# Token-first input stage and fp32 scan state in a one-core decoder trunk

## The chip, the cores and the metric

The kernel runs on one core of a Trainium2 chip, as a single launch. The time is that of the device, in microseconds (us), from start to end of one execution; the number given for the kernel before is the median of three runs, 1500.3 us (1499.67 to 1504.1). The profile is one further execution, recorded by the hardware profiler. TensorE multiplies matrices, VectorE, ScalarE and GpSimd work on rows of tiles, SyncE only issues DMA transfers. Tiles lie in on-chip memory as 128 partitions by a free dimension; TensorE's results lie in a small accumulator memory of banks, each 128 x 512 fp32.

## What is computed

x has 1024 tokens of 1024 channels. One Mamba-2 layer, then one attention layer, both conditioned by a vector c of 1024 numbers. Cut to the two places of the change, input modulation and chunked scan:

```python
def _modulate(x, g, shift, scale):
    return _rmsnorm(x, g) * (1.0 + scale[:, None, :]) + shift[:, None, :]

c_act = jax.nn.silu(c)
shift, scale, gate = jnp.split(c_act @ ada_w[i] + ada_b[i], 3, axis=-1)
h = _modulate(x, norm_g[i], shift, scale)        # rmsnorm: x / sqrt(mean over channels of x*x + eps)
zxbcdt = h @ in_w                                # z 2048, x/B/C 3072 (conv + silu), dt 32
...
def step(state, inp):                            # one chunk of 128 tokens; 4 groups of 8 heads of 64
    xc, ac, bc, cc = inp
    acum = jnp.cumsum(ac, axis=1)
    seg = jnp.where(causal, acum[:, :, None] - acum[:, None, :], -jnp.inf)
    scores = jnp.einsum('btgn,bsgn->btsg', cc, bc)[..., None] * jnp.exp(seg)
    y_diag = jnp.einsum('btsgh,bsghp->btghp', scores, xc)
    y_off = jnp.einsum('btgn,bghpn->btghp', cc, state) * jnp.exp(acum)[..., None]
    w_end = jnp.exp(acum[:, -1:] - acum)
    new_state = (state * jnp.exp(acum[:, -1])[..., None, None]
                 + jnp.einsum('bsgn,bsghp->bghpn', bc, xc * w_end[..., None]))
    return new_state, y_diag + y_off
```

Behind the scan come skip, gate by silu(z), a norm per group of 512 channels, the output projection, one projection to keys and values, stick-breaking attention and a last norm.

## The kernel before

**Numbers in two halves.** A projection in full accuracy runs as three products in the type fp32r (mm3, L129 to L132): an operand is split into a high half (the value rounded to fp32r) and a low half (value minus high), and high by high, low by high and high by low are added in one accumulator bank. Where an operand is plain fp32, a product is one instruction in the program and two records in the trace.

**First stage (L156 to L329).** x comes transposed (xT: tiles of 128 channels by 512 tokens, name x, sixteen of them, eight for each half of the tokens, hf). For the norm, ScalarE squares a tile (squares, L210), VectorE adds pairs (square_add, L215), and TensorE multiplies by a matrix of ones (square_sum, L219, bank ssx), which leaves the sum over channels in every partition; a logarithm, an exponential and three VectorE steps of 512 columns make the row of 1/rms (rms, L140 to L147, tile rbx). GpSimd multiplies each x tile by this row (scaled, L251). c goes through SiLU as an 8 x 128 tile, out to a buffer in memory (c_d) and back as a row crow, the same in all 128 partitions. For each of eight channel tiles d, gemv (L227) makes shift and scale with two VectorE products of 128 x 1024 that sum as they go (tile a0, 1 MB each by DMA); bias (L246, L248) finishes them with two one-column steps of ScalarE. Then high (L257, L260) makes the modulated tile hx and its high half h0h on ScalarE, and low (L265) the low half h0l on VectorE. With both halves of a tile, wave_mm runs nine products (three column tiles by three) into the banks prw; the weights (ww) are split by split_w (L233 on ScalarE, L234 on VectorE for d = 0, on GpSimd for the others). In this stage the order of TensorE, VectorE, ScalarE and GpSimd is the order in which the code is written (manual_schedule, L177). All of SyncE's transfers wait in the order of the program.

**Convolution stage.** The other 21 column tiles of the projection run over all 1024 tokens (bank pr, line 130 and following); its first product needs every tile of the first stage.

**Scan (L446 to L649).** 32 chunks: 8 units (a half of the tokens by a group g) of 4 chunks each. The four groups of the first half go first, then those of the second. For the chunk that comes next, chunk_a loads lm and eb, makes lm = exp of the decays on ScalarE, transposes x (px) and B (pb), multiplies B by C into the second part of pb, and forms xd = x * dt and lm = lm * scores on VectorE. chunk_c makes xw = x * w_end, splits it (xwh, xwl) and splits the transposed B (bsh, bsl). chunk_b runs on TensorE the state product (ps, three fp32r products), yo from the state st, and yd, eight small fp32 products; VectorE multiplies yo by eb, and the state becomes st * decay (GpSimd, in place) + ps (VectorE, L563). The last steps of a unit are gate (L576: skip, L581, gate by sz, squares) and norm_store (L594). Between these, TensorE works on the projection z of the next unit (zproj, 8 steps of three products, bank pz). In this stage only TensorE's order is that of the code (L456); the order of the other engines comes from the scheduler. px, ps, yo and yd have one accumulator bank each, pb two.

## Time and profile before

| | us |
|---|---|
| median of three runs | 1500.3 |
| lowest, highest | 1499.67, 1504.1 |
| the profiled execution, own time | 1502.42 |
| its span, first to last instruction | 1500.7 |
| TensorE busy in the span | 1435.7 (96%) |
| VectorE, ScalarE, GpSimd busy | 991.1, 742.3, 582.6 |
| granted TensorE clock, mean | 0.988 |

The span runs from the first to the last recorded instruction; the execution's own time has 1.7 us more around it. The program goes through its stages one behind the other: first stage to 90.15 us, convolution to 359.8, scan to 624.9, then a stretch of 48.9 us in which the output projection begins, then the rest. Busy shares of the whole span are means over these; a stage is read from its own window. The granted clock is a share of TensorE's full speed, 2.4 GHz; the lower level, 1.2 GHz, stands as about 0.5.

### The profile page before, as it was taken

The page shows a single profiled execution, that of the slowest core. Times are in us where ns is not written, and L with a number is a line of the kernel's source. Part 1 is how long each engine was busy: PE and PEld are TensorE (multiplying, and loading weights), DVE is VectorE, ACT ScalarE, POOL GpSimd, SP SyncE. Part 2 cuts the span into 40 slices and gives each one's busy share as a digit, 9 for nine tenths or more (in the row PEclk, how much of TensorE's full clock was granted, in tenths as well). Part 3 has the DMA queues.
Part 4 walks back from the last instruction along what each step waited for, and adds up shares of the span by engine and source line. Part 5 has one row for each costly group of instructions (what it writes and reads, how often), then busy time and mean ns, then how long its engine had stood idle before and what let it go on. Part 6 is the DMA issues. An engine that isn't in the chain of part 4 may idle for free.

```text
span 1500.7 us, 20592 instructions
## 1 busy us (share of the span) xinstructions
PE 1435.7 (96%) x7538; PEld 1115.1 (74%) x7538; DVE 991.1 (66%) x1221; ACT 742.3 (49%) x1249; POOL 582.6 (39%) x645
## 2 busy tenths in 40 slices
PE   4799999999998999999999999999999999999997
PEld 2587887888876778878888888876666666666797
DVE  5989975455789888886643526416666666668564
ACT  5554346224667666744432424325545455556452
POOL 2821220001654666443111000027666666667532
PEclk8899999999999999999999999999999999999999
DMA  9268885224576666657533446450212211112253
GB/s 333 95 235 295 288 288 170 98 99 122 176 229 198 220 199 210 226 179 264 176 125 124 136 129 194 138 178 33 66 43 64 63 57 39 61 57 78 79 189 106
DMA packets 104581, 227.36 MB, mean 152 GB/s; under 512 B 9488, under 2 KB 40992, under 8 KB 103456
## 3 DMA queue, kind: packets, MB, share of 16 engines
q1 hardware_dynamic: 104480, 226.04, 45.7%
q8 instruction: 60, 0.98, 0.3%
q14 instruction: 41, 0.34, 0.1%
HBM read 184.32 MB, written 41.68 MB: 151 GB/s over the span
## 4 chain that ended last, share of the span: by engine, by line
PE 73%; DVE 5%; ACT 2%; DMA 2%; issue 1%; POOL 1%; DVEq 0%; SPq 0%; POOLq 0%; ACTq 0%
PE sc L835 5%; PE av L888 4%; PE at L867 4%; PE po L132 4%; PE po L130 4%; PE po L131 4%; PE pz L130 2%; PE pqz L130 2%; PE pq L130 2%; PE pz L132 2%; PE pz L131 2%; PE pr L132 2%; PE pq L132 2%; PE pr L130 2%; PE pr L131 2%; PE pq L131 2%
## 5 line engine op out<-in xcount | busy, mean ns | idle before, releaser
L858 POOL TENSOR_TENSOR be<-be,kp 128x1024 f32<-128x1024 f32 (+2 forms) x96 | 162.3, 1691 | 90.2 <-DVE kp L852 70.9
L838 ACT ACTIVATE kp<-sc 128x1024 f32<-128x1024 f32 (+2 forms) x96 | 75.5, 813 | 174.6 <-PE sc L835 172.0
L852 DVE TENSOR_TENSOR_SCAN kp<-kp,pone 128x128 f32<-128x128 f32 (+3 forms) x128 | 96.1, 803 | 69.2 <-POOL kp L845 69.2
L130 PE MATMUL pr<-h0h,hx 128*128 128x512 f32 x336 | 132.3, 394 | 5.0 <-ACT hx L124 2.7
L132 PE MATMUL pr<-h0h,lx 128*128 128x512 f32 x336 | 132.3, 394 | 0.7 <-DVE lx L125 0.7
L131 PE MATMUL pr<-h0l,hx 128*128 128x512 f32 x336 | 131.9, 393 | 0.0
L505 ACT ACTIVATE lm<-lm,nac 128x128 f32<-128x128 f32 x256 | 78.6, 389 | 61.5 <-POOL lm L502 61.4
L130 PE MATMUL pz<-h0h,hz 128*128 128x512 f32 x256 | 105.5, 412 | 0.0
L131 PE MATMUL po<-yl,ho 128*128 128x512 f32 x256 | 100.8, 394 | 1.2 <-DVE yl L665 1.2
L132 PE MATMUL po<-yh,lo 128*128 128x512 f32 x256 | 100.4, 392 | 1.3 <-DVE lo L125 1.3
L132 PE MATMUL pz<-h0h,lz 128*128 128x512 f32 x256 | 100.4, 392 | 1.2 <-DVE lz L125 1.2
L131 PE MATMUL pz<-h0l,hz 128*128 128x512 f32 x256 | 99.9, 390 | 0.0
L130 PE MATMUL po<-yh,ho 128*128 128x512 f32 x256 | 99.9, 391 | 0.0
L852 DVE TENSOR_TENSOR_SCAN kp<-kp,ab,pone 128x512 f32<-128x512 f32 x64 | 78.4, 1266 | 28.3 <-ACT kp L838 17.2
L125 POOL TENSOR_TENSOR lq<-rq,hq 128x256 fp32r<-128x256 f32 x32 | 22.4, 730 | 178.4 <-ACT hq L124 178.4
L533 POOL TENSOR_TENSOR xwl<-xw,xwh 128x512 fp32r<-128x512 f32 x20 | 27.4, 1368 | 160.7 <-ACT xwh L531 156.2
L835 PE MATMUL sc<-kd,q 64*128 64x512 f32 (+3 forms) x384 | 81.5, 522 | 0.8 <-ACT be L839 0.8
L340 DVE SCALAR_TENSOR_TENSOR cv<-pr,vt,cv 128x1023 f32<-128x1023 f32 (+2 forms) x63 | 80.4, 1278 | 0.9
L130 PEld LDWEIGHTS pr<-h0h,hx 128*128 128x128 f32 x336 | 63.8, 190 | 18.9 <-ACT hx L124 3.1
L124 ACT CAST ho<-ro 128x1024 fp32r<-128x1024 f32 x32 | 33.7, 1054 | 89.1 <-PE po L131 79.2
L353 POOL TENSOR_TENSOR ar<-ar,crow 128x1024 f32<-128x1024 f32 x12 | 30.9, 2572 | 119.5 <-DMA ar<-adar 119.5
L867 PE MATMUL at<-ident,be 128*128 128x128 f32 x576 | 74.7, 272 | 1.1 <-DVE aT L877 1.1
(259 smaller groups left out, 3951.7 us busy)
## 6 DMA issues: line engine op xcount, KB each, us to landing
ar<-adar SPq DMA_DIRECT2D x48, 512.0 KB, 5.0
lm<-ac_d SPq DMA_DIRECT2D x32, 512.0 KB, 4.5
rz<-wz SPq DMA_DIRECT2D x32, 512.0 KB, 3.7
ro<-wmo SPq DMA_DIRECT2D x32, 512.0 KB, 3.5
xs_d<-sv SPq DMA_DIRECT2D x24, 512.0 KB, 3.8
rx<-wxbc SPq DMA_DIRECT2D x21, 512.0 KB, 4.7
x<-xT SPq DMA_DIRECT2D x32, 256.0 KB, 5.6
a<-ada SPq DMA_DIRECT2D x8, 1024.0 KB, 7.7
```

Of the source, the lines that this page charges most:

```text
L124: S.copy(h[:, i:i + n, :], r[:, i:i + n, :])
L130: E.matmul(ps, wh, xh, start=first, stop=False)
L131: E.matmul(ps, wh, xl, start=False, stop=False)
L132: E.matmul(ps, wl, xh, start=False, stop=last)
L340: V.scalar_tensor_tensor(out=ac[:, i:], in0=ps[:, :T - i], scalar=vv("cw", m * 4 + 3 - i), in1=ac[:, i:], op0=ALU.mult, op1=ALU.add)
L505: S.activation(lm[:, h, :], lm[:, h, :], AF.Exp, bias=nac[:, c, h0_ + h:h0_ + h + 1])
L835: E.matmul(ps[:, a, o:o + w], q[hsl[a], i * P:(i + 1) * P], kd[hsl[a], HT * c:HT * c + w], start=True, stop=True)
L838: S.activation(kp[:, :, ok:ok + w], ps[:, :, o:o + w], AF.Sigmoid, scale=-0.125)
L852: V.tensor_tensor_scan(out=ka, data0=ka, data1=pone.to_broadcast([P, w]), initial=1.0 if top else above[p, i][:, a, 0:1], op0=ALU.mult, op ...
L858: Q.tensor_tensor(out=be[:, :, o:o + w], in0=be[:, :, o:o + w], in1=kp[:, :, ok + 1:ok + w + 1], op=ALU.mult)
L867: E.transpose(ps[:, j, :], be[:, a, j * P:(j + 1) * P], ident)
L888: E.matmul(ps[hsl[a], cs], vd[:, j, hsl[a]], at[j // 4][:, a, j % 4, cs], start=j == 0, stop=j == nj - 1)
```

## The change

It touches two stages; the stages behind them keep their code and order.

**First stage.** x comes as it is, in tiles of 128 tokens by 1024 channels (xN, new input; names x0 to x7). A token is a partition, so the sum of squares of a token is one instruction with a running sum (squares: even tiles on ScalarE, odd on VectorE), 1/rms is a column of 128 x 4 for each half, and scaled multiplies a whole tile by a column, on VectorE and ScalarE in turn. GpSimd no longer works in this stage. After scaling, turn transposes four 128 x 128 blocks on TensorE into a bank, from which high reads. c is broadcast directly into crow, 512 KB, as the second transfer, and SiLU is taken on the whole row. spin puts products of raw x with the identity on TensorE, whose result is never read. The order of the loop over d is written anew, and split_w is VectorE's everywhere.

**Scan.** The state product is one fp32 product of the unsplit xw and B; xw has two tiles in turn and is made in chunk_a, as is the copy of B. The new state goes through a separate tile sd = st * decay on GpSimd. In chunk_b the order is now yd, yo, state product.

```diff
-        Y.dma_start(out=c8, in_=c)
-        S.activation(c8, c8, AF.Silu)
...
+        load_x(range(1))
+        Y.dma_start(out=crow, in_=c.rearrange("j p -> (j p)").partition_broadcast(P))
+        load_x(range(1, CPH))
...
+        def squares(t):
+            sq = tp.tile([P, D], F32, tag="sq", name=f"sq{t}", bufs=2)
+            acc = ssq[:, t // CPH, t % CPH:t % CPH + 1]
+            if t % 2:
+                V.scalar_tensor_tensor(out=sq, in0=xn[t], scalar=1.0, in1=xn[t], op0=ALU.mult,
+                                       op1=ALU.mult, accum_out=acc)
+            else:
+                S.activation(sq, xn[t], AF.Square, accum_out=acc)
...
+        def spin(x, m):
+            for i in range(m):
+                E.matmul(wave[NW - 1][:, HT:], ident, x, start=True, stop=True)
...
+            inv_rms(ssq[:, hf], rst[:, hf], rtt[:, hf], D)
...
+        def scaled(t):
+            r = rst[:, t // CPH, t % CPH:t % CPH + 1]
+            if t % 2:
+                V.tensor_scalar(out=xn[t], in0=xn[t], scalar1=r, scalar2=None, op0=ALU.mult)
+            else:
+                S.activation(xn[t], xn[t], AF.Identity, scale=r)
...
-        def scaled(d, hf):
-            Q.tensor_tensor(out=xt[d][hf], in0=xt[d][hf], in1=rbs[hf], op=ALU.mult)
...
+        def turn(d, hf):
+            ps = mm_tile(f"xp{d}_{hf}")
+            for i in range(CPH):
+                E.transpose(ps[:, i * P:(i + 1) * P], xn[hf * CPH + i][:, d * P:(d + 1) * P], ident)
+            xps[d, hf] = ps
...
+        squares(0)
+        squares(1)
+        S.activation(crow, crow, AF.Silu)
...
+        for t in range(2, CPH):
+            squares(t)
+        for t in range(CPH):
+            spin(xn[t][:, 0:HT], 2 if t == 0 else 1)
         rms(0)
+        for t in range(CPH):
+            scaled(t)
+        turn(0, 0)
+        turn(1, 0)
+        spin(xn[0][:, 0:HT], 3)
+        split_w(0, V)
         gemv(0)
...
+        unit(0, 0)
         wave_mm(0, 0)
+        spin(xn[0][:, 0:HT], 3)
+        for t in range(CPH, NC_):
+            squares(t)
+        rms(1)
+        for t in range(CPH, NC_):
+            scaled(t)
+        turn(0, 1)
...
         for d in range(2, ND):
...
+            unit(d, 0)
+            turn(d, 1)
+            if d + 1 < ND:
+                gemv(d + 1)
+                split_w(d + 1, V)
+            wave_mm(d, 0)
+            unit(d, 1)
+            if d + 1 < ND:
+                turn(d + 1, 0)
+                bias(d + 1)
+            wave_mm(d, 1)
...
-                xh = py.tile([P, 512], F32R, tag="xwh", name="xwh" + n, bufs=1)
-                xl = py.tile([P, 512], F32R, tag="xwl", name="xwl" + n, bufs=1)
-                S.copy(xh, xw)
...
+                sp["bs"] = py.tile([P, P], F32, tag="bs", name="bs" + n)
+                S.copy(sp["bs"], pb[:, 0:P])
...
+            yd = ppt.tile([P, 4, P], F32, tag="yd", name="yd" + n)
...
+                sd = py.tile([P, HPG, 64], F32, tag="sd", name="sd" + n, bufs=1)
+                Q.tensor_tensor(out=sd, in0=st[g].rearrange("p (h k) -> p h k", k=64), op=ALU.mult,
+                                in1=eev[:, c, hsl].unsqueeze(2).to_broadcast([P, HPG, 64]))
...
+                E.matmul(ps, sp["bs"], sp["xw"], start=True, stop=True)
...
+                    V.tensor_tensor(out=st[g], in0=ps, in1=sd.rearrange("p h k -> p (h k)"), op=ALU.add)
```

Here unit(d, hf) is high followed by low.

**VectorE in the first stage, around d = 1 and 2.** The names are h0l (low half, channel tile and token half), a0 (weights of shift and scale), wwl (low half of the wave weights). Before:

```order
L265 TENSOR_TENSOR h0l1_0_346<-hx0_1_0_343,h0h1_0_345 128x512
L227 SCALAR_TENSOR_TENSOR a0_2_218,mod_127<-a0_2_218,crow_157 128x1024 x2
L265 TENSOR_TENSOR h0l0_1_365<-hx0_0_1_362,h0h0_1_364 128x512
L265 TENSOR_TENSOR h0l1_1_386<-hx0_1_1_383,h0h1_1_385 128x512
L227 SCALAR_TENSOR_TENSOR a0_3_222,mod_127<-a0_3_222,crow_157 128x1024 x2
L265 TENSOR_TENSOR h0l2_0_409<-hx0_2_0_406,h0h2_0_408 128x512
L265 TENSOR_TENSOR h0l2_1_425<-hx0_2_1_422,h0h2_1_424 128x512
L227 SCALAR_TENSOR_TENSOR a0_4_226,mod_127<-a0_4_226,crow_157 128x1024 x2
```

After:

```order
L234 TENSOR_TENSOR wwl1_313<-ww1_194,wwh1_312 128x384
L227 SCALAR_TENSOR_TENSOR a0_1_192,mod_126<-a0_1_192,crow_156 128x1024 x2
L268 TENSOR_TENSOR h0l0_1_319<-hx0_0_1_316,h0h0_1_318 128x512
L268 TENSOR_TENSOR h0l1_0_338<-hx0_1_0_335,h0h1_0_337 128x512
L234 TENSOR_TENSOR wwl2_347<-ww2_198,wwh2_346 128x384
L227 SCALAR_TENSOR_TENSOR a0_2_196,mod_126<-a0_2_196,crow_156 128x1024 x2
L268 TENSOR_TENSOR h0l1_1_364<-hx0_1_1_361,h0h1_1_363 128x512
L268 TENSOR_TENSOR h0l2_0_386<-hx0_2_0_383,h0h2_0_385 128x512
L227 SCALAR_TENSOR_TENSOR a0_3_200,mod_126<-a0_3_200,crow_156 128x1024 x2
```

The splits of the wave weights stand now on VectorE, and one gemv stands between the two low halves of the tile before its own, no longer two tiles ahead.

**GpSimd in the first stage.** Names as above; rbx is the row of 1/rms, ar the later modulation weights. Before:

```order
L251 TENSOR_TENSOR x0_0_175<-x0_0_175,rbx0_242 128x512
L251 TENSOR_TENSOR x1_0_177<-x1_0_177,rbx0_242 128x512
L234 TENSOR_TENSOR wwl1_338<-ww1_216,wwh1_337 128x384
L251 TENSOR_TENSOR x0_1_176<-x0_1_176,rbx1_243 128x512
L251 TENSOR_TENSOR x1_1_178<-x1_1_178,rbx1_243 128x512
L234 TENSOR_TENSOR wwl2_378<-ww2_220,wwh2_377 128x384
L251 TENSOR_TENSOR x2_0_179<-x2_0_179,rbx0_242 128x512
L251 TENSOR_TENSOR x2_1_180<-x2_1_180,rbx1_243 128x512
```

After, from the end of the constants on:

```order
masks.py:199 ISA
masks.py:199 AFFINE_SELECT ident_58<-ident_58 128x128
L163 AFFINE_SELECT tri_157<-ones_63 128x128
L363 TENSOR_TENSOR ar0_3_1058<-ar0_3_1058,crow_156 128x1024
L363 TENSOR_TENSOR ar0_7_1071<-ar0_7_1071,crow_156 128x1024
```

Nothing stands any more between the triangle tri and the first slice of the late weights.

**TensorE in the scan, one chunk (group 1, chunk 1).** pz is the projection of the next unit. Before:

```order
L132 MATMUL pz2_0_1_2945<-h0h5_0_533,lz2_0_1_2942 128x512
L130 MATMUL ps1_1_2991<-xwh1_1_2924,bsh1_1_2928 128x512
L131 MATMUL ps1_1_2991<-xwl1_1_2925,bsh1_1_2928 128x512
L132 MATMUL ps1_1_2991<-xwh1_1_2924,bsl1_1_2929 128x512
L553 MATMUL yo1_1_2995<-ct1_0_2465,st1_2285 128x128 x4
L566 MATMUL yd1_1_3003<-lm1_1_2871,xd1_1_2895 64x128 x8
L130 MATMUL pz2_0_1_2945<-h0h6_0_573,hz2_0_1_2941 128x512
```

After:

```order
L131 MATMUL pz2_0_1_2930<-h0h5_0_534,lz2_0_1_2927 128x512
L545 MATMUL yd1_1_2980<-lm1_1_2864,xd1_1_2888 64x128 x8
L555 MATMUL yo1_1_2991<-ct1_0_2487,st1_2313 128x128 x4
L560 MATMUL ps1_1_2997<-xw1_1_2890,bs1_1_2892 128x512
L129 MATMUL pz2_0_1_2930<-h0h6_0_582,hz2_0_1_2926 128x512
```

yd has moved ahead of yo, and the state product from the front to the end, as one product.

**VectorE in the scan, at the end of a unit (group 2) and the start of the next (group 3).** yl are low halves for the output projection, lz of the z weights. Before:

```order
L514 TENSOR_TENSOR xd3_1_3701<-px3_1_3693,dtv_146 128x512
L525 TENSOR_TENSOR xw3_1_3728<-px3_1_3693,wdv_147 128x512
L516 TENSOR_TENSOR lm3_1_3677<-pb3_1_3698,lm3_1_3677 128x1024
L581 SCALAR_TENSOR_TENSOR y2_0_2854<-xg2_0_2847,vt_67,y2_0_2854 128x512 x4
L665 TENSOR_TENSOR yl4_0_5503<-yr4_0_5542,yh4_0_5502 128x512
L569 COPY y3_0_3257<-yd3_0_3718 128x4x128
L533 TENSOR_TENSOR xwl3_1_3731<-xw3_1_3728,xwh3_1_3730 128x512
L665 TENSOR_TENSOR yl5_0_5505<-yr5_0_5546,yh5_0_5504 128x512
L537 TENSOR_TENSOR bsl3_1_3735<-pb3_1_3698,bsh3_1_3734 128x128
```

After:

```order
L124 TENSOR_TENSOR lz0_1_1_3675<-rz0_1_1_3672,hz0_1_1_3674 128x1024
L524 TENSOR_TENSOR xd3_1_3636<-px3_1_3628,dtv_145 128x512
L529 TENSOR_TENSOR xw3_1_3638<-px3_1_3628,wdv_146 128x512
L578 SCALAR_TENSOR_TENSOR y2_0_2847<-xg2_0_2840,vt_67,y2_0_2847 128x512 x4
L566 COPY y3_0_3221<-yd3_0_3652 128x4x128
L659 TENSOR_TENSOR yl4_0_5331<-yr4_0_5370,yh4_0_5330 128x512
L534 TENSOR_TENSOR lm3_1_3612<-pb3_1_3633,lm3_1_3612 128x1024
L124 TENSOR_TENSOR lz0_1_2_3759<-rz0_1_2_3756,hz0_1_2_3758 128x1024
```

lm of chunk 1 stood ahead of the four products of the skip (y2_0, line 581 before) and now stands behind them, behind the copy y3_0 and a low half; the subtractions xwl and bsl are gone.

## Rows read from the trace of the kernel before

The columns of a window row are its bounds, its length, busy us and instruction count of TensorE, its weight load, VectorE, ScalarE and GpSimd, the granted clock, the DMA share and GB/s.

**Rows 1.** Windows: us; busy us (instructions) per engine; clock; DMA.

```profile
0.00:90.15 90.15, 60.39 (x192) 39.07 (x193) 66.28 (x73) 51.00 (x87) 44.75 (x33) 0.89 0.61 218
...
359.80:624.90 265.10, 250.89 (x1547) 203.19 (x1546) 224.97 (x277) 175.77 (x384) 151.17 (x107) 0.99 0.63 200
624.90:673.80 48.90, 46.42 (x281) 37.47 (x280) 44.30 (x56) 26.62 (x49) 21.01 (x14) 1.00 0.62 200
```

**Rows 2.** Windows of ten us of the first stage.

```profile
20.00:30.00 10.00, 5.38 (x7) 2.33 (x8) 8.77 (x14) 5.55 (x11) 3.47 (x2) 0.52 1.01 377
...
40.00:50.00 10.00, 6.49 (x20) 4.74 (x20) 10.00 (x10) 5.71 (x11) 10.00 (x6) 0.83 0.43 142
```

**Rows 3.** One of TensorE's waits, first stage: us in total, times, longest.

```profile
PE prw L131 <- DVE h0l L265: 9.1, 5, 2.9
```

**Rows 4.** TensorE's waits, 359.8 to 624.9 us.

```profile
PE ps L130 <- DVE st L563: 6.6, 6, 2.8
PE ps L131 <- DVE xwl L533: 2.9, 2, 2.8
PE ps L132 <- DVE bsl L537: 1.4, 2, 1.1
```

**Rows 5.** Groups by line, first stage: count | busy us, mean ns | idle before.

```profile
L227 DVE SCALAR_TENSOR_TENSOR a<-a,crow 128x1024 f32<-128x1024 f32 x16 | 28.6, 1824 | 0.0
L265 DVE TENSOR_TENSOR h0l<-hx,h0h 128x512 fp32r<-128x512 f32 x16 | 20.5, 1312 | 1.4 <-ACT h0h L260 1.4
```

**Rows 6.** Timeline, first stage, three engines: start, us, engine, line, operation.

```profile
2.64 1.28 ACT L166 ACT_TABLE_LOAD   x1
...
7.82 3.98 ACT L210 ACTIVATE sq<-x 128x512 f32<-128x512 f32 x6 [1.76 <-DMA x<-xT]
...
24.62 6.18 PE L219 MATMUL ssx<-sq,ones 128*128 128x512 f32 x8 [9.23 <-DVE sq L215]
...
72.89 1.21 DVE L227 SCALAR_TENSOR_TENSOR a<-a,crow 128x1024 f32<-128x1024 f32 x1
...
74.03 1.22 DVE L227 SCALAR_TENSOR_TENSOR a<-a,crow 128x1024 f32<-128x1024 f32 x1
...
75.30 0.39 ACT L246 ACTIVATE mod<-mod,vt 128x1 f32<-128x1 f32 x1 [0.41 <-DVE a L227]
...
75.96 0.82 ACT L257 ACTIVATE hx<-x,mod 128x512 f32<-128x512 f32 x1
...
77.52 0.68 DVE L265 TENSOR_TENSOR h0l<-hx,h0h 128x512 fp32r<-128x512 f32 x1
```

**Rows 7.** A group of small steps (by line), 90 to 360 us.

```profile
L361 DVE TENSOR_TENSOR mod<-mod,vt 128x8 f32<-128x8 f32 x4 | 0.6, 160 | 1.3 <-ACT ar L354 1.3
```

**Rows 8.** Timeline of TensorE at four places.

```profile
37.22 0.63 PE L130 MATMUL prw<-h0h,wwh 128*128 128x512 f32 x1
37.64 0.63 PE L131 MATMUL prw<-h0l,wwh 128*128 128x512 f32 x1
...
90.16 0.39 PE L130 MATMUL pr<-h0h,hx 128*128 128x512 f32 x1
90.38 0.40 PE L131 MATMUL pr<-h0l,hx 128*128 128x512 f32 x1
...
538.75 1.02 PE L597 MATMUL rs<-sq,ones 128*128 128x512 f32 x2
...
539.84 0.40 PE L131 MATMUL ps<-xwl,bsh 128*128 128x512 f32 x1
...
545.84 0.60 PE L508 MATMUL px<-ident,xg 128*128 128x128 f32 x4
```

**Rows 9.** Timeline of the scan, VectorE and TensorE.

```profile
476.68 4.81 DVE L581 SCALAR_TENSOR_TENSOR y<-xg,vt,y 128x512 f32<-128x512 f32 x4
...
549.67 1.09 PE L566 MATMUL yd<-lm,xd 128*64 128x128 f32 x16
...
558.73 1.09 PE L566 MATMUL yd<-lm,xd 128*64 128x128 f32 x16
```

More of the change, by code (lines that the diff above doesn't have):

```diff
@@ L281, in tile_trunk @@
                                op1=ALU.mult)
-        split_w(0, V)
-        squares(1, 0, 2)
         bias(0)
-        square_add(1, 0, 2)
-        square_sum(1, 0, 2)
-        high(0, 0)
-        low(0, 0)
-        squares(1, 4, 6)
-        square_add(1, 4, 6)
-        square_sum(1, 4, 6)
-        wave_mm(0, 0)
+        unit(0, 0)
+        wave_mm(0, 0)
+        spin(xn[0][:, 0:HT], 3)
[5 more added lines that the diff above has]
+        turn(0, 1)
+        split_w(1, V)
+        high(0, 1)
         gemv(1)
-        rms(1)
-        split_w(1, Q)
+        low(0, 1)
         bias(1)
-        high(1, 0)
-        low(1, 0)
-        scaled(0, 1)
-        scaled(1, 1)
-        wave_mm(1, 0)
-        gemv(2)
-        high(0, 1)
-        low(0, 1)
-        wave_mm(0, 1)
-        split_w(2, Q)
-        scaled(2, 0)
-        scaled(2, 1)
-        high(1, 1)
-        low(1, 1)
+        wave_mm(0, 1)
+        unit(1, 0)
+        turn(1, 1)
+        split_w(2, V)
+        gemv(2)
+        wave_mm(1, 0)
+        unit(1, 1)
+        turn(2, 0)
+        bias(2)
         wave_mm(1, 1)
-        gemv(3)
-        split_w(3, Q)
         for d in range(2, ND):
-            bias(d)
-            for hf in range(NH):
-                high(d, hf)
-                if d + 1 < ND:
-                    scaled(d + 1, hf)
-                low(d, hf)
-                wave_mm(d, hf)
-            if d + 2 < ND:
-                gemv(d + 2)
-                split_w(d + 2, Q)
+            unit(d, 0)
[9 more added lines that the diff above has]
+            wave_mm(d, 1)
             if d == 4:
@@ L546, in chunk_b @@
             ysl = u["y"][:, :, cs]
-            if c < NC_ - 1:
-                ps = ppt.tile([P, 512], F32, tag="ps", name="ps" + n)
-                mm3(ps, *sp["bs"], *sp["xw"], True, True)
+            yd = ppt.tile([P, 4, P], F32, tag="yd", name="yd" + n)
+            for h in range(HPG):
+                E.matmul(yd[64 * (h % 2):64 * (h % 2) + 64, h // 2, :], xd[:, h, :], lm[:, h, :],
+                         start=True, stop=True)
+            if 0 < c < NC_ - 1:
+                sd = py.tile([P, HPG, 64], F32, tag="sd", name="sd" + n, bufs=1)
+                Q.tensor_tensor(out=sd, in0=st[g].rearrange("p (h k) -> p h k", k=64), op=ALU.mult,
+                                in1=eev[:, c, hsl].unsqueeze(2).to_broadcast([P, HPG, 64]))
             if c > 0:
@@ L556, in chunk_b @@
             if c < NC_ - 1:
+                ps = ppt.tile([P, 512], F32, tag="ps", name="ps" + n)
+                E.matmul(ps, sp["bs"], sp["xw"], start=True, stop=True)
                 if c == 0:
@@ L559, in chunk_b @@
                 else:
-                    s3 = st[g].rearrange("p (h k) -> p h k", k=64)
-                    Q.tensor_tensor(out=s3, in0=s3, op=ALU.mult,
-                                    in1=eev[:, c, hsl].unsqueeze(2).to_broadcast([P, HPG, 64]))
-                    V.tensor_tensor(out=st[g], in0=ps, in1=st[g], op=ALU.add)
-            yd = ppt.tile([P, 4, P], F32, tag="yd", name="yd" + n)
-            for h in range(HPG):
-                E.matmul(yd[64 * (h % 2):64 * (h % 2) + 64, h // 2, :], xd[:, h, :], lm[:, h, :],
-                         start=True, stop=True)
+                    V.tensor_tensor(out=st[g], in0=ps, in1=sd.rearrange("p h k -> p (h k)"), op=ALU.add)
             if c == 0:
```

83 lines of the change are left out of this document (24 added, 59 removed).

## The prediction

> **What bounds the kernel now.** I read the table of windows first, cut at the program's stages, then the waits of the stage in question, then single instructions in the timeline. The reader is to see three things. In the first 90 us TensorE is busy for 60 us at a mean clock of 0.89 [rows 1], although nothing later can start without it; in this stage VectorE and GpSimd are both busy without a break (10.00 of 10.00 us, [rows 2]), and TensorE waits for squares (9.23 us in front of its first sum alone, [rows 6]) and for the low halves of the input (9.1 us, [rows 3]). In the scan, from 359.8 to 624.9 us, TensorE is busy 251 of 265 us and VectorE 225 [rows 1]: it is close to TensorE's own work, and what is lost is lost in front of the state product, 6.6 us for the previous state, 2.9 us for the low half of xw, 1.4 us for the low half of B [rows 4]. All else in the program keeps its order on every engine, so I count only these two stages. Both end in a dense TensorE: what they save moves everything behind them.
>
> **First stage, removed.** Eight sums of squares on TensorE in fp32, and their waits; GpSimd's sixteen multiplications by the row of 1/rms and seven splits of weights. GpSimd then has nothing to do here until the first slice of the late modulation weights. That matters for VectorE: beside a busy GpSimd its 1024-wide product averaged 1824 ns and the low half 1312 ns [rows 5], while alone, at 72.89 us and 77.52 us, they took 1.21 and 0.68 us [rows 6]. I price every VectorE step of this stage at the second pair. Started one behind the other, the 1024-wide ones are 1.15 us apart (72.89 to 74.03), the 512-wide ones some 0.6.
>
> **First stage, added.** A square per token tile, a scaling per token tile, 64 transposes, eleven spare products, and the new chain. Worked out in order of time:
> - In the kernel before, the first half of x (2.1 MB) has landed by about 11.1 us, when the last square of its six starts (7.82 plus 3.98 less one of 0.66, [rows 6]). Now the 0.5 MB of c goes out ahead of three quarters of it; at the 377 GB/s of [rows 2] that is 1.4 us, so I take 12.0 us, between 11.1 and 12.5. The round trip of c through memory is gone, but its row is wanted at 17.6 us only, so I give that nothing.
> - c's SiLU is now 1024 wide and stands on ScalarE in front of the square of tile 2, with a table load of 1.28 us behind it (2.64, [rows 6]). c lies in the first 1.0 MB of the queue; 0.75 MB had landed by 7.82 [rows 6], so 8.5 at 377 GB/s, and 1.3 + 1.28 + 1.3 more end at 12.4, while VectorE's square of the tile that lands last ends at 13.2: hidden by 0.8 us, and beyond that each us costs one.
> - Square of the last tile 1.2; two small ScalarE steps 0.66 (as from 75.30 to 75.96, [rows 6]) and three small VectorE steps of 0.16 [rows 7]; two scalings on ScalarE, 1.1 each (512 columns take 0.66 in the six of 7.82, [rows 6], twice that is the most); the split of the first weights about 1.0: 17.6 us. Then two 1024-wide products 2.37, a small step 0.16, and from the bias to the start of the low half 2.22 (75.30 to 77.52 [rows 6], bias, modulation, cast): first low half at 22.4 us.
> - The second half is scaled only then: two squares behind the low half 3.0, 1/rms 1.1, two scalings 2.2, split 1.0, products 2.4, bias to low 2.2: the next d at 34.4, and with 0.6 + 0.5 + 2.4 + 2.2 the low half of d=2 starts at 40.1 us.
> - From there one turn of the loop is low half 0.6, products 2.4, bias to low 2.2, so 5.2 us. TensorE's share of a turn is 18 products at 0.228 (90.16 to 90.38, [rows 8]) and 8 transposes at 0.11 (four in 0.60 with a last one of 0.27, [rows 8]), 5.0 us: hidden, by 0.2 us only; were the loop faster it would be the bound. Five turns, 0.4 for the dt weights and 1.0 for one more cast: the last d at 67.6 us, and the second low half of d=6 ends at 65.4.
> - From that point TensorE has 8 + 32 + 18 products and four transposes left, 13.7 us: the first product of the convolution stage at 79.1 us. Before it was at 90.16 [rows 8]. **Term: 11 us less.** Its ends: 77 with a landing at 11.1 and turns of TensorE's 5.0 us; 85 with a landing at 14, 0.1 us more in each of five hand-overs of a turn and on the way in, so 5 to 13 us.
>
> The spare products cost time only where they stand in front of work that is ready. Five run on raw x before 1/rms exists; three stand behind the first transposes (17.3 us) and end, even at 0.86 x 2 us each, at 22.4 us, when the first modulated tile comes; three stand behind the first wave products, and end at 28 us where the next transposes come at 29. So nothing; if cover fails, 2.6 us a group.
>
> **Scan, removed.** The three waits above, 10.9 us [rows 4]; each of their ten restarts also costs the 0.16 us by which a product's duration (0.39) exceeds its distance to the next (0.23), together 12.5 us. ScalarE's casts of xw and VectorE's and GpSimd's two subtractions go as well; they lie off the path. **Added.** The state product is one fp32 product instead of three. An fp32 product of 512 columns holds TensorE 0.86 us (the norm's one starts at 538.75 and the second product behind it at 539.84, less one of 0.23, [rows 8]), three at 0.228 hold it 0.68: 0.17 more, 28 times, 4.8 us, and it is on the path. That path is real: two neighbouring chunks without a wait are 9.06 us apart (549.67 to 558.73, [rows 9]), and their own products sum to 8.7.
>
> **Scan, moved.** yd now opens a chunk. Queued behind it on TensorE are yo, the state product and the next projection, so a late lm or an unread yd bank stops all of them. The dangerous place is the unit in the order above: lm of chunk 1 now stands behind the four products of the previous unit's skip, 4.81 us [rows 9]. From eb of the previous unit's last chunk to that lm VectorE has eight steps of 0.6, two of 1.15 and the four: 11.9 us. TensorE, from that chunk's yo to this yd, has two state products, one yd, 42 projection products and two sets of transposes: 15.1 us. VectorE enters about 2.5 us late because of the four norm products before, so it just holds. The state sum now has from one state product to the next chunk's yo, some 7 us, and its GpSimd factor no longer waits for yo. I take 1 us of new waits, near nothing, because the same steps in front of it lose the subtractions; the ends are 0 and the whole 12.5, a wait that only changes its name. **Term: 12.5 - 4.8 - 1 = 7 us less**, between 8 less and 5 more; and at best 3.3 less still with the rest of the stretch's idle time (265.1 - 250.9 - 10.9) and 2.5 with that of the unit behind it (48.9 - 46.4, [rows 1]).
>
> **Sum.** The profiled execution took 1502.4 us; 1502.4 - 11 - 7 = 1484.4. It stands 2.1 us above the median of the runs, 1500.3, so the forecast against the median is 1482.
>
> **A rule against it.** In the profile the clock was 0.52 from 20 to 30 us [rows 2], and TensorE had stood still for 9.23 us up to 24.62 [rows 6]; where it ran at its lower level, 1.2 GHz, neighbouring products were 0.42 us apart (37.22 to 37.64, [rows 8]). The Trainium skill, TensorE: Matmul & The Clock Gate, Part 4 (PE-mode transpose), states that transposes do not lift the clock the way products do. By that rule the loop's 64 transposes would do nothing to hold the clock up. No run here shows such a loop; the sum by it is that of the rival "cold" below, the sum by the rows is the forecast.
>
> **Rivals.**
> - *The waits change their name* (12 in 100): yd waits for lm or for its bank as long as the state product waited. For it: VectorE is busy 225 of 265 us [rows 1]. Against it: it loses work. Then the scan is 5 us longer: 1500.3 - 11 + 5 = 1494.
> - *The loop stays slow* (10 in 100): its turns keep the contended prices, 2 x 1.82 and 1.31 with 2.2 of ScalarE, about 7.2 us, so 2.0 more in each of five. For it: DMA fills memory all the while. Against it: GpSimd is empty. 1500.3 - 1 - 7 = 1492.
> - *It doesn't do what it says* (6 in 100): both of these at once, near 1502.
> - *Cold, the slower side* (4 in 100): TensorE runs the whole loop at its lower level. A turn is then 18 x 0.42 + 0.9 = 8.5 us, 3.3 more in each of eight turns; 26 us later against 18 saved: 1508. It decides from 7.5 us a turn on. For it: the clock of [rows 2]. Against it: TensorE has 5.0 us of work in 5.2.
> - *More than counted* (8 in 100): turns of 5.0 us and the small waits gone: 1500.3 - 13 - 8 - 3 - 2.5 = 1474.
>
> **How the numbers follow.** The forecast, 1482, has 60 in 100 and reaches by its ends from 1475 to 1491. The slower end takes in the first two rivals, at 1494 and 1492, each with 2 us for the first stage's own spread; the faster end the last one, with 2 us likewise. So 1472 to 1496; what is left out is the one that does nothing, the cold one, and the tails. A run of this kernel can tell 0.3%, 4.5 us, from no change. Faster than 1495.8: the forecast, more than counted, and nearly all of the first two rivals, 0.85; slower than 1504.8: cold, and a part of the one that does nothing, 0.05; the rest 0.10.
>
> **What would show it.** The first convolution product near 79 us; low halves of 0.68 us and turns of 5.2 us between 40 and 66; GpSimd idle there; the clock at its full level from about 25 us. In the scan no TensorE wait over 1 us in front of the state product, chunks 9.2 us apart, and waits at yd of a microsecond in all. Wrong would be: a clock at its lower level inside the loop, turns over 6 us, or several us of waits at yd on lm.

## The result, and the profile after

The changed kernel takes 1478.5 us (median of four executions, 1474.9 to 1481.9) against 1500.5 for the kernel before: ratio 0.985, 95% interval 0.982 to 0.988. The profiled execution took 1481.9 us with a span of 1480.2, 20.5 us less than the span before.

The windows of the changed kernel, cut at the first convolution product, the first projection product of the scan stage and the first product of the output projection (columns as in [rows 1]):

```profile
0.00:80.90 80.90, 66.16 (x266) 44.72 (x267) 44.41 (x79) 50.96 (x85) 1.12 (x9) 0.96 0.60 225
80.90:325.38 244.48, 235.94 (x1020) 193.35 (x1019) 174.50 (x192) 102.93 (x130) 34.81 (x15) 0.98 0.62 215
325.38:608.19 282.81, 281.37 (x1675) 219.95 (x1673) 231.47 (x265) 178.32 (x379) 135.04 (x91) 1.00 0.62 203
```

The same cuts in the kernel before stand at 90.16, 331.56 and 627.41 us. So the first stage lost 9.3 us, the convolution stage became 3.1 us longer (241.4 to 244.5), the scan 13.0 us shorter (295.85 to 282.81), and all behind it 1.3 shorter. In the first stage GpSimd's 44.75 us of [rows 1] are 1.12.

VectorE in the first stage by line, which answers [rows 5]: the same two groups, now on an empty GpSimd.

```profile
L227 DVE SCALAR_TENSOR_TENSOR a<-a,crow 128x1024 f32<-128x1024 f32 x16 | 18.9, 1218 | 0.0
L268 DVE TENSOR_TENSOR h0l<-hx,h0h 128x512 fp32r<-128x512 f32 x16 | 11.0, 689 | 14.4 <-ACT h0h L263 14.2
```

The 1824 and 1312 ns of [rows 5] became 1218 and 689, the prices of [rows 6] that the prediction took.

VectorE's timeline, the first low half of all and then that of the first token half of channel tiles 2 to 6:

```profile
20.67 0.69 DVE L268 TENSOR_TENSOR h0l<-hx,h0h 128x512 fp32r<-128x512 f32 x1 [2.10 <-ACT h0h L263]
...
40.47 0.69 DVE L268 TENSOR_TENSOR h0l<-hx,h0h 128x512 fp32r<-128x512 f32 x1 [2.49 <-ACT h0h L263]
...
45.55 0.69 DVE L268 TENSOR_TENSOR h0l<-hx,h0h 128x512 fp32r<-128x512 f32 x1 [1.03 <-ACT h0h L263]
...
51.55 0.69 DVE L268 TENSOR_TENSOR h0l<-hx,h0h 128x512 fp32r<-128x512 f32 x1 [1.94 <-ACT h0h L263]
...
56.80 0.69 DVE L268 TENSOR_TENSOR h0l<-hx,h0h 128x512 fp32r<-128x512 f32 x1 [0.86 <-ACT h0h L263]
...
62.34 0.69 DVE L268 TENSOR_TENSOR h0l<-hx,h0h 128x512 fp32r<-128x512 f32 x1 [1.50 <-ACT h0h L263]
```

A turn is 5.1 to 6.0 us, 5.5 in the mean. TensorE's timeline in the same stage:

```profile
29.23 0.51 PE L129 MATMUL prw<-h0h,wwh 128*128 128x512 f32 x1 [1.52 <-ACT h0h L263]
...
31.15 0.80 PE L130 MATMUL prw<-h0l,wwh 128*128 128x512 f32 x1 [1.42 <-DVE h0l L268]
31.75 0.63 PE L131 MATMUL prw<-h0h,wwl 128*128 128x512 f32 x1
...
32.17 0.63 PE L129 MATMUL prw<-h0h,wwh 128*128 128x512 f32 x1
...
37.16 0.39 PE L130 MATMUL prw<-h0l,wwh 128*128 128x512 f32 x1
...
37.39 0.39 PE L131 MATMUL prw<-h0h,wwl 128*128 128x512 f32 x1
```

Behind the two waits of 1.5 and 1.4 us the products stand 0.42 to 0.43 us apart (the lower level, 1.2 GHz), until some 36.9 us, then 0.23.

TensorE's waits of the changed kernel, first the scan stage (which answers [rows 4]), then the convolution stage:

```profile
PE yd L545 <- DVE lm L534: 0.8, 1, 0.8
PE rs L594 <- POOL sq L586: 0.6, 1, 0.6
```

```profile
PE pr L129 <- ACT hx L123: 4.0, 1, 4.0
PE pr L129 <- DVE cv L350: 3.1, 2, 2.2
PE pr L131 <- DVE lx L124: 1.4, 1, 1.4
```

Of the 10.9 us in front of the state product nothing is left; 0.8 us came at yd, on lm. The 0.6 us at the norm's sum is not new (see the rows of the kernel before in the next section but one). One chunk on TensorE, start, duration, line and operation:

```profile
548.37 1.09 PE L545 MATMUL yd<-lm,xd 128*64 128x128 f32 x16
549.39 1.16 PE L555 MATMUL yo<-ct,st 128*128 128x128 f32 x8
550.38 1.02 PE L560 MATMUL ps<-xw,bs 128*128 128x512 f32 x2
550.85 0.80 PE L129 MATMUL pz<-h0h,hz 128*128 128x512 f32 x1
551.48 0.39 PE L130 MATMUL pz<-h0l,hz 128*128 128x512 f32 x1
```

From the state product to the second projection product are 1.10 us; less one product of 0.23, it holds TensorE 0.87 us.

### The profile page after: what moved, and what is told of

Read it like the earlier page. It is cut to its first block, busy times and chain, and to the rows that moved or that the text cites. A ratio compares the mean times of both kernels' runs of the same rounds, so it can differ in the third digit from the quotient of the medians.

```text
span 1480.2 us, 20539 instructions
## 1 busy us (share of the span) xinstructions
PE 1442.3 (97%) x7580; PEld 1112.3 (75%) x7580; DVE 957.2 (65%) x1196; ACT 726.7 (49%) x1218; POOL 520.4 (35%) x602
## 4 chain that ended last, share of the span: by engine, by line
PE 78%; DVE 3%; DMA 1%; ACT 1%; issue 1%; POOL 0%; DVEq 0%; SPq 0%; POOLq 0%; ACTq 0%
PE sc L829 5%; PE av L882 5%; PE at L861 4%; PE po L131 4%; PE po L130 4%; PE po L129 4%; PE pz L131 3%; PE pz L129 3%; PE pz L130 3%; PE pqz L129 2%; PE pq L129 2%; PE pr L131 2%; PE pq L131 2%; PE pr L129 2%; PE pr L130 2%; PE pq L130 2%
## 5 line engine op out<-in xcount | busy, mean ns | idle before, releaser
L129 PE MATMUL pz<-h0h,hz 128*128 128x512 f32 x256 | 113.0, 441 | 0.0
L550 POOL TENSOR_TENSOR sd<-st,eev 128x512 f32<-128x512 f32 x24 | 39.4, 1641 | 133.7 <-ACT st L562 121.0
L124 POOL TENSOR_TENSOR lq<-rq,hq 128x256 fp32r<-128x256 f32 x32 | 22.4, 730 | 177.8 <-ACT hq L123 177.8
L350 DVE SCALAR_TENSOR_TENSOR cv<-pr,vt,cv 128x1023 f32<-128x1023 f32 (+2 forms) x63 | 80.3, 1277 | 0.9
L512 POOL TENSOR_SCALAR_AFFINE_SELECT lm<-lm 128x1024 f32<-128x1024 f32 x32 | 40.3, 1260 | 113.2 <-DMA lm<-ac_d 84.4
```

Source lines behind the costliest of these rows:

```text
L129: E.matmul(ps, wh, xh, start=first, stop=False)
L350: V.scalar_tensor_tensor(out=ac[:, i:], in0=ps[:, :T - i], scalar=vv("cw", m * 4 + 3 - i), in1=ac[:, i:], op0=ALU.mult, op1=ALU.add)
L512: Q.affine_select(out=lm, in_=lm, pattern=[[0, HPG], [1, P]], compare_op=ALU.is_ge, fill=-1e30, base=0, channel_multiplier=-1)
```

## The experiments

The table gives one profiled execution of each kernel, us between the cuts above, read from TensorE's timeline.

| kernel | first convolution product | convolution stage | scan | rest |
|---|---|---|---|---|
| before | 90.2 | 241.4 | 295.9 | 873.3 |
| changed | 80.9 | 244.5 | 282.8 | 872.0 |
| after_again | 80.2 | 236.7 | 284.2 | 874.4 |
| first_only | 79.8 | 235.7 | 294.2 | 875.7 |
| scan_only | 89.3 | 238.4 | 285.0 | 872.6 |
| no_spin | 80.5 | 233.3 | 282.1 | 871.9 |
| no_spin_2 | 79.6 | 236.8 | 281.9 | 872.4 |
| move_ns | 80.0 | 235.6 | 287.5 | 875.5 |
| type_ns | 80.0 | 237.6 | 284.8 | 871.6 |
| spin_hold | 80.2 | 235.9 | 281.6 | 873.4 |
| ada_dve | 79.1 | 230.5 | 283.1 | 873.1 |
| ada_dve_spin | 79.6 | 230.5 | 283.6 | 874.5 |
| pool_load | 97.9 | 240.0 | 281.6 | 872.4 |

**after_again: the changed kernel once more.**

> The changed kernel once more, for its spread and a second profile. In its first profile TensorE ran at its lower level from 31.15 to 36.87 us (14 products 0.42 us apart where 0.23 is usual), some 2.7 us. Theory: this stretch, which hangs on two waits for VectorE of 1.4 to 1.5 us ahead of it, is there in some executions only and makes part of the 7 us between its fastest and slowest (1474.9 to 1481.9): the median stays at 1476 to 1481. Rival: the stretch is there in every execution and the spread comes from later stages (transfers of the convolution stage), then the first convolution product is again at 80.9 us.

1477.3 us (1471.9 to 1481.0), ratio 0.988 (0.985 to 0.990). The lower level between 30 and 37 us was there again and the first convolution product at 80.2, so the spread is not from this stage: that much of the rival holds. What is seen in the convolution stage is a wait for VectorE, though, not for the transfers that the rival named. Ten-us windows of this execution:

```profile
110.00:120.00 10.00, 6.74 (x25) 5.18 (x24) 10.00 (x12) 6.54 (x7) 1.17 (x1) 0.87 0.60 203
120.00:130.00 10.00, 10.00 (x44) 8.22 (x43) 10.00 (x14) 2.51 (x5) 2.41 (x1) 0.96 1.04 378
```

TensorE stands still for 3.3 us for VectorE's convolution, and the clock is below full for two windows. In the first profile of this kernel such falls stood at 120 to 140 and 230 to 250 us, behind a wait of 2.2 us for VectorE and one of 4.0 for ScalarE. Over the nine executions of this kernel the time goes with the mean granted clock: 0.991 to 0.993 in the four above 1480 us, 0.995 and 0.996 in the two below 1475.

**first_only and scan_only: either part alone.** Lines of the scan (L513 to L571 before) or of the first stage are those of the kernel before.

```diff
 first_only:
+                mm3(ps, *sp["bs"], *sp["xw"], True, True)
...
-                E.matmul(ps, sp["bs"], sp["xw"], start=True, stop=True)
 scan_only:
-                mm3(ps, *sp["bs"], *sp["xw"], True, True)
...
+                E.matmul(ps, sp["bs"], sp["xw"], start=True, stop=True)
```

> The first stage of the changed kernel with the scan of the kernel before. Theory: the first convolution product comes at 80.9 us (9.3 earlier than before), some 3 us of it are given back in the convolution stage, where TensorE's waits add up to 8.5 us in place of 6.4, and nothing of the rest is lost: 1500.5 - 6 = 1494.5. Rival 'kept': the 3 us are chance of one execution, 1491.5. Rival 'given back': the convolution stage is bound by its transfers and takes the whole gain, 1500.

> The first stage of the kernel before with the scan of the changed one. Theory: the scan is 13 us shorter, since the losses in front of the state product were 17.6 us in all and not the 12.5 that the prediction counted: 1500.5 - 13 = 1487.5, chunks 9.25 us apart, no wait over 1 us in front of the state product. Rival: the scan's gain is the prediction's 7 us (1493.5), and the other 6 us in the changed kernel come from the earlier start of everything.

first_only: 1487.8 us, ratio 0.995 (0.993 to 0.997); scan_only: 1485.5, ratio 0.993 (0.992 to 0.995). Against the 1496.9 of the kernel before in these rounds that is 9.1 and 11.4 us; together 20.5, and the changed kernel had 19.7 less. The parts add up. The expectations were reckoned from 1500.5 us; as differences, 9.1 us is what the rival 'kept' said (9), and 11.4 lies nearer to the theory's 13 than to the rival's 7. The first stage's 9 to 11 us are kept: the 3 us given back in the first profile belong to that execution, for here the convolution stage is 235.7 us. The scan alone is 10.8 us shorter than before in the stage table, between the prediction's 7 and the 13 expected. TensorE's waits in the scan of first_only:

```profile
PE ps L129 <- DVE st L573: 5.7, 5, 2.8
PE pz L131 <- DVE lz L124: 1.7, 1, 1.7
PE ps L131 <- DVE bsl L547: 1.4, 2, 1.1
PE ps L130 <- DVE xwl L543: 1.2, 1, 1.2
```

The waits of [rows 4] stand there again, with the clock at 0.67 to 0.93 in three ten-us windows of the stage.

**no_spin: without the spare products; no_spin_2: the same again.**

```diff
-        for t in range(CPH):
-            spin(xn[t][:, 0:HT], 2 if t == 0 else 1)
...
-        spin(xn[0][:, 0:HT], 3)
...
-        spin(xn[0][:, 0:HT], 3)
```

> The changed kernel without its eleven spare products. Theory: they cost nothing and bring little, since between 26.1 and 31.2 us TensorE waits and falls to the lower level even with them, and the loop is dense behind it: 1477 to 1481, first convolution product between 80 and 83 us. Rival: they are what brings the loop to the full clock; without them it runs at the lower level up to 40 us or beyond, each turn then 8.5 us in place of 5.4, so 3 us or more a turn: 1484 or more, first convolution product behind 86 us.

> The kernel without spare products once more, since its 6 us over the changed kernel do not come from the first stage (first convolution product 80.5 us against 80.2 and 80.9) but from the convolution stage and the scan, where their code is the same. Theory 'spares': it is faster again, 0.983 of the kernel before within 0.002, about 1470 to 1473. Rival 'chance of the executions': it falls among those of the changed kernel, 0.985 to 0.988, 1475 to 1480.

1471.3 us, ratio 0.983 (0.982 to 0.985), and then 1474.9, ratio 0.986 (0.984 to 0.988); the changed kernel had 0.985 and 0.988. The first convolution product stays at 80.5 and 79.6 us: in the first stage the spare products buy nothing and cost nothing. Without them the wave products run at the lower level from their first one on, 0.43 us apart, up to 36.7 us, and it does not matter, because TensorE waits for the chain of VectorE and ScalarE there anyway. Both expectations for no_spin were too slow; the second result lies between the theory's 1470 to 1473 and the rival's 1475 to 1480, and its ratio is in the rival's range. Whether the spare products cost something later is not settled: the first six us were half gone the second time, two of its five executions took 1480 us, and in its profile the clock fell in the convolution stage too (0.83 from 110 to 120 us) and the stage took 236.8 us, as in after_again. One more thing is seen in no_spin, in the convolution stage: GpSimd and VectorE side by side.

```profile
85.31 3.23 POOL L359 TENSOR_TENSOR ar<-ar,crow 128x1024 f32<-128x1024 f32 x1 [83.55 <-DVE ar L362]
```

```profile
86.19 3.43 DVE L362 SCALAR_TENSOR_TENSOR ar<-ar,crow 128x1024 f32<-128x1024 f32 x1
...
89.56 1.27 DVE L346 SCALAR_TENSOR_TENSOR cv<-rw,vt,cv 128x1022 f32<-128x1022 f32 x1
```

A VectorE product that takes 1.22 us elsewhere lasts 3.43 and ends about a microsecond behind GpSimd's.

**pool_load: work for GpSimd in the first stage.** The added products feed nothing.

```diff
+            if d >= 2:
+                for _ in range(2):
+                    Q.tensor_tensor(out=tp.tile([P, HT], F32, tag="gs", name=f"gs{d}_{hf}_{_}", bufs=1),
+                                    in0=f(h0[d][hf][0]), in1=xn[0][:, 0:HT], op=ALU.mult)
```

> The changed kernel without spare products, and with GpSimd given work in the loop of the first stage again: two 512-wide products for each modulated tile from the third channel tile on, into a tile that nothing reads. Theory 'GpSimd' (the prediction's price of the emptied GpSimd): VectorE's 1024-wide products go from 1.22 to 1.8 us in the mean and the low halves from 0.69 to about 1.3, a turn from 5.4 to 7 us; first convolution product 8 to 10 us later, near 90, whole time 1479 to 1482. Rival 'memory': VectorE was slow in the kernel before for other reasons (transfers, its operands), nothing changes: 80.5 us and 1471.

1494.2 us, ratio 0.998 (0.997 to 0.999): nearly the whole gain of the kernel is gone. The first convolution product comes at 97.9 us, against 80.5 in no_spin and 90.2 in the kernel before. VectorE and GpSimd by line, 35 to 95 us:

```profile
L227 DVE SCALAR_TENSOR_TENSOR a<-a,crow 128x1024 f32<-128x1024 f32 x11 | 20.6, 1903 | 0.0
L272 DVE TENSOR_TENSOR h0l<-hx,h0h 128x512 fp32r<-128x512 f32 x13 | 16.3, 1260 | 8.2 <-ACT h0h L263 8.2
L234 DVE TENSOR_TENSOR wwl<-ww,wwh 128x384 fp32r<-128x384 f32 x5 | 5.9, 1181 | 0.0
```

```profile
L266 POOL TENSOR_TENSOR gs<-h0h,x 128x512 f32<-128x512 f32 x24 | 41.0, 1707 | 48.0 <-ACT h0h L263 44.1 <-ACT an L414 2.4
```

The prices of [rows 5] are back, to within 80 ns, on the new code and with transfers nearly still. The theory's mechanism holds and the rival 'memory' does not; the size was too small, 17.4 us measured for 8 to 10. I had counted the two products and one low half of a turn; two low halves and the split belong to it. For the steps in the rows above that is 11 x (1.90 - 1.22) + 13 x (1.26 - 0.69) + 5 x (1.18 - 0.55) = 18.0 us. TensorE waited 15.4 us for low halves in this stage, 1.8 in no_spin; its clock fell in these waits (0.83 to 0.93 in four ten-us windows from 40 us on), and how much of the 17.4 us is due to that is not separated.

The Trainium skill, SBUF — State Buffer, section "SBUF: two separate sides", states that VectorE and GpSimd take turns at a pair of ports for a whole instruction when the VectorE step has two operands in on-chip memory. This case agrees: the products and subtractions above have two such operands and are held. The 60 convolution steps of no_spin that read an accumulator bank took 1277 ns in the mean, and 1280 in ada_dve, where GpSimd makes no products; 14 of the 60 ran beside a product of GpSimd, and none of these took more than 1283 ns. One of them, and the step behind it, which reads one operand and has it in on-chip memory:

```profile
99.45 2.47 POOL L359 TENSOR_TENSOR ar<-ar,crow 128x1024 f32<-128x1024 f32 x1 [10.91 <-DMA ar<-adar]
```

```profile
99.57 1.27 DVE L346 SCALAR_TENSOR_TENSOR cv<-pr,vt,cv 128x1023 f32<-128x1023 f32 x1
100.77 1.31 DVE L407 TENSOR_SCALAR dtu<-dtu 128x256 f32<-128x256 f32 x1
```

The convolution step runs through; the next one, 0.29 us in ada_dve, ends 0.16 us behind GpSimd's product. So a step with a single operand can be held too.

**ada_dve: GpSimd's products of the convolution stage given to VectorE; ada_dve_spin: that with the spare products.**

```diff
-ADAP = 4
+ADAP = 16
```

> The changed kernel without the spare products, with the twelve 1024-wide products of the late modulation weights that GpSimd made in the convolution stage given to VectorE, so that GpSimd makes none there. Theory: beside such a GpSimd product (2.4 to 3.4 us) a VectorE step that reads on-chip memory alone is held (3.43 us for one of 1.21, 3.22 for another), so VectorE loses more to GpSimd's help than the 1.15 us that each product costs it, and the wait of 2.5 us for the convolution at 113.7 us goes or shrinks below 1: 1467 to 1471. Rival: 12 x 1.15 = 14 us more on a VectorE that is busy without a break from 80 to 116 us, the wait grows: 1473 to 1478.

> The changed kernel with its spare products and GpSimd's twelve products of the late weights on VectorE (1467.3 without the spare products). Theory 'behind waits': what the changed kernel loses against the one without spare products is lost where TensorE's clock falls behind waits of 2 to 4 us in the convolution stage; with the wait at 113 us gone the spare products cost nothing: 1466 to 1469, and no ten-us window of the convolution stage under a clock of 0.99. Rival 'spares': they cost 5 to 6 us whatever stands behind: 1472 to 1474.

ada_dve: 1467.3 us (1466.2 to 1468.5), ratio 0.980 (0.979 to 0.982), the fastest kernel here. ada_dve_spin: 1468.9 (1466.6 to 1471.4), ratio 0.981 (0.979 to 0.982). The convolution stage of no_spin, of no_spin_2 and of ada_dve, one window each:

```profile
80.52:313.79 233.27, 230.74 (x1021) 190.39 (x1019) 169.02 (x192) 103.19 (x130) 36.30 (x15) 1.00 0.63 225
79.57:316.33 236.76, 232.87 (x1020) 191.41 (x1019) 174.02 (x192) 103.02 (x130) 34.05 (x15) 0.99 0.63 222
79.10:309.55 230.45, 230.45 (x1020) 190.52 (x1019) 172.53 (x216) 87.99 (x104) 3.72 (x3) 1.00 0.66 228
```

In ada_dve TensorE is busy without a break at the full clock, 230.45 us, and the same in ada_dve_spin: both theories hold. ScalarE's twelve sums go as well. VectorE took twelve products more, 14 us of them, but its busy time rose by 3.5 only against no_spin (169.0 to 172.5) and fell by 1.5 against no_spin_2 (174.0): GpSimd's help had cost it 10 to 15 us by holding its other steps. Without the wait there is no fall of the clock in this stage, and with and without the spare products the times agree within their spread.

**move_ns and type_ns: order and type of the state product, one at a time.** Both without the spare products. Neither is quite alone: move_ns keeps the split halves, the single xw and the state scaled in place of the kernel before; type_ns keeps the second xw, the earlier copies and the tile sd of the changed one.

```diff
 move_ns:
-                E.matmul(ps, sp["bs"], sp["xw"], start=True, stop=True)
+                mm3(ps, *sp["bs"], *sp["xw"], True, True)
 type_ns (the product ahead of yo, yd behind it):
+            if c < NC_ - 1:
+                ps = ppt.tile([P, 512], F32, tag="ps", name="ps" + n)
+                E.matmul(ps, sp["bs"], sp["xw"], start=True, stop=True)
             if c > 0:
                 yo = ppt.tile([P, 4, P], F32, tag="yo", name="yo" + n)
```

> The changed kernel without the spare products (1471.3 in the run before), and in the scan only the change of TensorE's order: yd, yo, then the state product as three fp32r products from split halves as before; xw has one tile again, the state is scaled in place. Theory 'order': the place behind yo is what takes the losses in front of the state product away; with three products of 0.68 us in place of one of 0.86 it is 28 x 0.18 = 5 us faster than without this edit: 1464 to 1468, chunks 9.06 us apart, no wait over 1 us at the state product. Rival 'type': the subtractions for the low halves come back to VectorE and GpSimd and are as late as before, and the waits for them (5.2 us in the kernel before, with restarts some 8) return: 1475 to 1480.

> The changed kernel without the spare products, with the state product (one fp32 product) back in front of yo and yd as the last of a chunk. Theory 'order': the waits for the previous state come back (6.6 us and six restarts in the kernel before, some 8 us), those for low halves do not: 1477 to 1481. Rival 'type': with no halves to wait for nothing is lost, 1470 to 1473.

move_ns: 1483.0 us, ratio 0.991 (0.989 to 0.993). type_ns: 1476.8, ratio 0.987 (0.985 to 0.989). My theory of the order was wrong in both: move_ns is 15 us and more behind it and slower than its rival too, and in type_ns, whose time is at the edge of the theory's range, only 1.0 us of waits for the previous state came back; what it has over no_spin is in part in the convolution stage (237.6 us for 233.3). TensorE's waits in the scan, of move_ns and of type_ns:

```profile
PE yd L555 <- DVE y L576: 3.9, 2, 3.1
PE px L514 <- DVE xw L531: 2.2, 2, 1.5
PE yo L560 <- DVE st L572: 1.6, 2, 1.0
PE pb L516 <- DVE rt L145: 1.4, 1, 1.4
```

```profile
PE pz L131 <- DVE lz L124: 1.9, 1, 1.9
PE ps L541 <- ACT st L555: 1.0, 1, 1.0
```

Moved alone, the state product no longer waits for halves, but VectorE, which still makes them, is late everywhere else: the waits change their name, 9.1 us. With the type alone hardly a wait is left, although the product stands in front. Against the 294.2 us of first_only the scan is 6.7 us shorter with the order alone, 9.4 with the type alone, 12.2 with both, one profile each. Most of the gain comes with the type, that is with the subtractions taken off VectorE and GpSimd and the tiles that go with it, which no run here takes apart. What the order adds to it, 2.8 us, is not clear of the spread: over nine profiles with both edits the scan took 281.6 to 285.0 us, and type_ns took 284.8.

**spin_hold: the clock held up at 26 to 37 us.**

```diff
         turn(0, 1)
+        spin(xn[0][:, 0:HT], 2)
         split_w(1, V)
         high(0, 1)
+        low(0, 1)
         gemv(1)
-        low(0, 1)
```

> The changed kernel with its eleven spare products and two more in front of the second wave product, and with the low half of tile 0, second half, ahead of the modulation product of tile 1 on VectorE. Theory 'dense': the fall of TensorE's clock between 26 and 37 us hangs on the waits of 1.5 and 1.4 us there; with these filled or gone the stretch runs at the full level and the first convolution product comes 1.5 to 3 us earlier, at 78 to 79.5 us. Rival 'chain': this stretch is set by VectorE's and ScalarE's chain; at the full clock TensorE only waits more, and the first convolution product stays at 80 to 81 us. For the whole time either gives 1472 to 1480, since what differs in the convolution stage is larger.

1474.5 us, ratio 0.986 (0.984 to 0.988). Ten-us windows:

```profile
20.00:30.00 10.00, 8.56 (x26) 4.08 (x25) 6.37 (x13) 7.29 (x12) 0.00 (x0) 1.00 1.03 410
30.00:40.00 10.00, 7.43 (x33) 5.47 (x34) 6.40 (x12) 5.89 (x12) 0.00 (x0) 1.00 0.59 212
```

The clock is at its full level in both, the products from 30 to 37 us stand 0.23 us apart, and the first convolution product comes at 80.2 us all the same: the rival, a chain of VectorE and ScalarE, holds. The run changes two things at once, but no_spin, at the lower level there without either, says the same.

## Why the prediction was right, point by point

The forecast of 1482 us lies 3.5 us above the median, and its mechanism was the right one in both stages. Its two terms were off in opposite ways: 11 us for a measured 9.3 (9.3 to 10.6 over changed, after_again, first_only and ada_dve_spin, which have this first stage, against the one profile of before), and 7 us for a measured 13.0 in the first profile, 10.8 in scan_only. That the sum came so close is in part luck: in the first profile 1.7 us too much in one term, 6.0 too little in the other and 3.1 given back in a stage that was not counted.

- *VectorE's steps at the price of an empty GpSimd*: right, 1218 and 689 ns, and shown by pool_load, which takes it away again. It is not the whole of this term: of the 9.3 us 5.0 are there at the first low half already (25.69 us in the kernel before, 20.67 now), 4.2 come behind it.
- *The way in*: 20.67 us for the first low half, where 22.4 was worked out. The last tile of the first half was there 1.5 us earlier than the 12.0 taken: VectorE's square of it began at 10.46.
- *The low half of the third channel tile* at 40.47 us for 40.1: what the way in had gained was lost on the second half of the tokens, 19.8 us for the 17.7 worked out. *A turn* 5.5 us for 5.2; five of them, with the dt weights and one more cast, 27.8 us for 27.5. TensorE's share of 5.0 is nearly the whole of it, as the prediction saw (busy 9.4 to 9.8 of 10 us in the windows from 40 to 70 us). Of the 1.8 us by which 80.9 misses 79.1, 1.0 is there when the second low half of d = 6 ends (66.4 us for 65.4); the other 0.8 is TensorE's work behind it, 14.5 us for 13.7.
- *The clock at full level from about 25 us*: wrong. It was at the lower level from about 30 to 37, ahead of the loop, and by no_spin and spin_hold this cost nothing. In the loop behind, with eight transposes in each turn, it was 1.00 in each window from 40 us on and the products stood 0.23 us apart: the rival "cold" did not come. What transposes alone would do no run shows.
- *The spare products cost nothing*: right for their own stage. That they do anything for the kernel is not seen in any run here.
- *All behind moves by what the two stages save*: right in sum (first_only and scan_only add up), with one omission: the convolution stage is no fixed block. The prediction took it as unchanged; it was 233 to 245 us with a GpSimd product in each fourth step, by how long TensorE waited for VectorE and ScalarE and whether its clock then fell.
- *The scan's waits, 12.5 us*: this is the term that was mis-sized. Four more lines of the view that [rows 4] is taken from:

```profile
PE pz L132 <- DVE lz L125: 1.2, 1, 1.2
PE ps L131 <- POOL xwl L533: 0.9, 1, 0.9
PE rs L597 <- POOL sq L589: 0.6, 1, 0.6
PE px L508 <- DVE xw L525: 0.6, 1, 0.6
```

The second one is a wait in front of the state product that was not counted, and the list leaves short waits out. The 17.6 us of the expectation for scan_only sum, over all state products of the kernel before, the distances from the start of one product to the next beyond the usual 0.23; they contain five times 0.41 us behind the norm's fp32 product, which holds TensorE itself and was not lost. Taken against an undisturbed state product with the same product ahead of it, the loss from that product to the start of what follows is 15.9 us, the lower clock behind the longest wait for the state (2.8 us) included. With the two waits for lz and xw, 1.8 us, which are gone too, less 28 x 0.18 = 5.0 for the fp32 product and 0.8 at yd, that makes 11.9 us; measured were 13.0, 11.7 and 10.8 in the changed kernel, after_again and scan_only.
- *The fp32 product, 0.17 us more*: 0.87 measured against 3 x 0.23, so 0.18; chunks 9.25 us apart for 9.2. *New waits, 1 us*: 0.8 at yd, on lm, in the place that the prediction named; the 0.6 at the norm's sum was there before.
- *Why the waits went*: the prediction left open which edit took them. type_ns shows that the fp32 product, with the subtractions it saves VectorE and GpSimd and the tiles that go with it, does most; move_ns shows the rival "the waits change their name" at work when only the order is changed.
- *Both of the first two rivals at once, near 1502*: by their own terms 1500.3 - 1 + 5 = 1504; it changes nothing above.

Still open: why the clock falls behind some waits and not behind others of the same length. In the convolution stage it fell behind waits of 2.22 (changed), 2.47 (no_spin_2), 2.66 (move_ns) and 3.26 us (after_again and first_only), and not behind 2.27 (type_ns), 2.53 (no_spin) and 2.70 us (spin_hold). So it is open, too, whether the 2 to 7 us between the changed kernel and the one without spare products are the spare products' or chance.

## What to carry to other kernels

Before an idle engine is given work, look at what its work does to its neighbour: here GpSimd's products cost VectorE 10 to 15 us where they took 14 off it; giving them to VectorE was worth 3 to 6 us in one stage, and giving GpSimd work in another cost 17. Size a wait that is to be removed by the distances of starts in that place, against one that was not disturbed, and not by the list of waits (15.9 us here for 10.9), and add what the clock loses behind it. A wait for a late engine moved to other instructions here when only the order was changed (9.1 us in move_ns); take work off the late engine first.

## What the runs showed of the hardware that was not expected

- The granted clock reads 1.00 in the windows from 20 to 40 us of no_spin, though its products there stand 0.43 us apart up to 36.7 us: the column showed no lower level there, and the distance of products has to be read beside it. The first record of the clock in that trace begins at 36.9 us.
- A VectorE step held beside GpSimd can take nearly three times its time (3.43 us for 1.22), while steps that read an accumulator bank are not held at all (at most 1283 ns in 14 of them beside GpSimd, 1280 in the mean without it). A step with one operand was held as well (1.31 us for 0.29).
- In the same code TensorE's clock fell in the convolution stage in some profiles and not in others, behind waits of the same length (2.47 and 2.53 us). The executions of these kernels spread over up to 9 us (1471.9 to 1481.0); without a wait in that stage four lay within 2.3 us (ada_dve) and 4.8 (ada_dve_spin).
